# Attention's product with v: plain fp32, two heads in the two column halves of the array, instead of high and low parts over the full array

## The chip, the cores and the metric

The kernel is one program on one core of a Trainium2 chip. The metric is the device time of one execution in microseconds (us); lower is better. A core has TensorE (PE in the profile, with its weight loads shown apart as PEld), VectorE (DVE), ScalarE (ACT), GpSimd (POOL) and a queue engine (SP) that issues transfers. Each engine works through its own list of instructions in the order in which the built program holds them.

## What is computed

Two layers of a diffusion backbone are computed for 128 prompt tokens and 512 sample tokens. Layer 0 is gated attention with 16 query heads and 4 key/value heads of 64 columns; layer 1 is a bidirectional state-space mixer, which the change doesn't touch. The part that matters:

```python
def attend(q, k, v):                      # 16 query heads, 4 kv heads, head_dim 64
    s = einsum('bqgrd,bsgd->bgrqs', qb, k) * scale
    p = softmax(s, axis=-1)
    return einsum('bgrqs,bsgd->bqgrd', p, v)
# prompt tokens see 128 keys; sample tokens see 128 cached keys and 512 own keys
yp = (attend(...) * silu(g)) @ w_out
```

## The kernel before

The tokens lie in five tiles of 128: tile 0 is the prompt, tiles 1 to 4 are the sample. Products are made in the format fp32r, with each operand split into a high part (a cast on ACT) and a low part (source minus high part, on DVE or POOL): `split` is lines 72 to 74, so that these casts and subtractions all bear the lines L73 and L74, and the tile's name tells them apart (`ph`, `pl` for turned probabilities, `qs` for queries, `wh`, `wl` for weights, `v` for v).

`attention` runs over the four kv groups. A group has nine units: four heads with query tiles 1 and 2, the prompt with all four heads, four heads with query tiles 3 and 4. A unit has a first half, `head_A`: the scores of one head and one query tile against all 640 keys (L630), the row maximum (L633, DVE), the exponential (L637, ACT). Its second half is `head_B`: the probabilities of both query tiles are turned in three steps of up to two key tiles each (L658, transposes into the PSUM tile `pt`, of which there are two), split into `ph` and `pl`, and multiplied with `v2` (L668). `v2` holds the high and the low part of v side by side, 2 x 64 columns, so that one matmul of 128 stationary columns makes both products; the two halves of the result lie on different partitions and `combine` (L567 on ACT, L568 on DVE) adds them. The prompt's unit does the same with 128 keys (L598, L606, L607). The gate is scaled, turned (L562) and multiplied in `post`.

The second half of a unit is written between the first half of the next one and other work, the "fill": projections of the next group's queries and of the gate (L283), modulation rows of both layers (L175, plain fp32 in column quarters of the array), and in the last group early pieces of the output projection (L841). The builder's scheduler then sets the final order on each engine; `order` below is that final order.

The array's column halves are used by this kernel already in layer 1, in `diag` (L1145): each program line there multiplies plain fp32 with 64 stationary columns, heads alternating between the two halves, eight matmuls to a tile and group, 160 in all.

## Time and profile before

| what | value |
|---|---|
| median of 3 runs | 988.72 us (988.35 to 992.33) |
| profiled execution, its own time | 996.43 us |
| its span in the trace | 994.6 us |
| granted TensorE clock over the span | 0.979 of full |
| attention's units, first score to last product with v | about 91 to 381 us |

A profiled execution is one execution with the hardware profiler on. Its time stands 7.7 us above the median of the runs, so that differences are worked out against its own rows and then set against the median. Busy times of PE are the union of bars; a bar holds the matmul's passage through the array and ends later than the next matmul may start, so that matmuls of one kind show their true cost in the distance from start to start.

### The profile page before, as it was taken

To read this page: it belongs to the slowest core of one execution; us is meant where nothing else is said; L and a number is where in the kernel's file an instruction comes from. 1 tells how busy PE (TensorE), PEld (TensorE's weight loads), DVE (VectorE), ACT (ScalarE), POOL (GpSimd) and SP (SyncE) were. 2 spreads that over 40 slices of the span, in tenths; PEclk is the share of its full clock that TensorE was granted. 3 is DMA by queue.
4 is the path that set the end of the run, shared out by engine and by line. 5 is a ranking of instruction groups with operands and counts; after the bars stand their busy time and mean duration, and the time that the engine had idled before them with its cause. 6 is when DMAs were issued, how large, how long until landed. Compare 5 with 4: busy or idle time off the path is not lost.

```text
span 994.6 us, 17413 instructions
## 1 busy us (share of the span) xinstructions
PE 933.1 (94%) x6578; PEld 845.7 (85%) x6578; DVE 663.8 (67%) x1046; ACT 517.4 (52%) x1208; POOL 411.8 (41%) x397
## 2 busy tenths in 40 slices
PE   5998999999999989989899989999999999989898
PEld 3887979979997779989799979799889899768686
DVE  4468666566675774884858776856686657898553
ACT  5345666667675763333446565456436552544340
POOL 3245235227271071364235676448543862332000
PEclk9899999999999999999999999999999999999899
DMA  9941253131114223333449766755476545456742
GB/s 307 348 143 50 84 165 128 47 103 36 29 44 128 85 66 109 124 107 89 128 139 264 199 197 198 183 181 157 155 206 189 183 132 160 145 180 206 256 161 101
DMA packets 121476, 146.98 MB, mean 148 GB/s; under 512 B 8688, under 2 KB 93808, under 8 KB 121392
## 3 DMA queue, kind: packets, MB, share of 16 engines
q1 hardware_dynamic: 110640, 140.62, 46.0%
q10 hardware_dynamic: 10752, 5.24, 1.8%
q8 instruction: 52, 0.85, 0.4%
q14 instruction: 32, 0.26, 0.1%
HBM read 128.73 MB, written 17.10 MB: 147 GB/s over the span
## 4 chain that ended last, share of the span: by engine, by line
PE 55%; DVE 16%; DMA 12%; issue 6%; POOL 5%; ACT 5%; SPq 1%; ACTq 0%; POOLq 0%; DVEq 0%
PE pj L914 15%; PE pp L283 8%; DMA am<-acd 5%; PE pj L1383 3%; PE po L668 3%; PE acc L379 3%; PE a L841 3%; PE S L630 3%; PE pt L658 3%; DVE wl L74 2%; DMA u<-yzd 2%; PE pp L175 2%; PE a L1383 2%; POOL am L1132 2%; PE a L1192 2%
## 5 line engine op out<-in xcount | busy, mean ns | idle before, releaser
L914 PE MATMUL pj<-h,wh 128*128 128x322 f32 (+1 forms) x1248 | 289.9, 319 | 10.0 <-DVE B L1006 4.5
L914 PEld LDWEIGHTS pj<-h,wh 128*128 128x128 f32 (+1 forms) x1248 | 210.8, 189 | 19.2 <-issue 12.0
L74 POOL TENSOR_TENSOR wl<-raw,wh 128x512 fp32r<-128x512 f32 (+1 forms) x70 | 134.9, 1938 | 178.7 <-ACT wh L73 178.4
L914 PE MATMUL pj<-h,wl 128*128 128x322 f32 (+1 forms) x624 | 200.6, 322 | 0.0
L73 ACT CAST wh<-raw 128x1024 fp32r<-128x1024 f32 (+1 forms) x117 | 103.2, 912 | 91.3 <-DMA raw<-in_l_w_out 27.9
L1131 ACT ACTIVATE am<-am,nb 128x128 f32<-128x128 f32 x320 | 98.1, 390 | 57.6 <-POOL am L1127 46.2
L914 PEld LDWEIGHTS pj<-h,wl 128*128 128x128 f32 (+1 forms) x624 | 118.4, 190 | 4.2 <-issue 3.8
L283 PE MATMUL pp<-wh,big 128*128 128x256 f32 x576 | 112.2, 285 | 0.5 <-ACT sg L527 0.5
L74 DVE TENSOR_TENSOR wl<-raw,wh 128x1024 fp32r<-128x1024 f32 x47 | 66.7, 1428 | 40.9 <-ACT wh L73 40.9
L283 PEld LDWEIGHTS pp<-wh,big 128*128 128x128 f32 x576 | 91.2, 188 | 0.9 <-ACT sg L527 0.7
L283 PE MATMUL pp<-wl,big 128*128 128x256 f32 x288 | 81.2, 282 | 0.0
L74 DVE TENSOR_TENSOR pl<-pt,ph 128x512 fp32r<-128x512 f32 (+1 forms) x100 | 59.2, 599 | 25.6 <-ACT ph L73 25.0
L633 DVE TENSOR_REDUCE nm<-S 128x1 f32<-128x640 f32 x64 | 52.4, 820 | 13.7 <-PE S L630 12.7
L73 ACT CAST ph<-pt 128x512 fp32r<-128x512 f32 (+1 forms) x100 | 51.4, 518 | 18.8 <-PE pt L658 14.1
L1132 POOL TENSOR_TENSOR am<-am,am 128x1024 f32<-128x1024 f32 x20 | 49.2, 2458 | 22.5 <-ACT am L1131 22.5
L637 ACT ACTIVATE Pt<-S,nm 128x640 f32<-128x640 f32 x64 | 51.3, 803 | 13.1 <-PE pt L658 9.5
L1383 PE MATMUL pj<-wh,h 128*128 128x512 f32 x160 | 54.0, 412 | 2.1 <-ACT wh L73 2.1
L283 PEld LDWEIGHTS pp<-wl,big 128*128 128x128 f32 x288 | 54.3, 188 | 0.0
L630 PE MATMUL S<-kT,qT 128*128 128x320 f32 x256 | 51.4, 326 | 2.3 <-ACT Pt L637 2.3
L658 PE MATMUL pt<-cst,Pt 128*128 128x128 f32 x320 | 50.7, 275 | 2.7 <-DVE pl L74 2.3
L1126 POOL TENSOR_SCALAR_AFFINE_SELECT am<-am 128x1024 f32<-128x1024 f32 x20 | 23.5, 1176 | 59.0 <-DMA am<-acd 51.5
L841 PE MATMUL a<-wh,big 128*128 128x256 f32 x256 | 46.8, 283 | 0.0
(345 smaller groups left out, 2114.9 us busy)
## 6 DMA issues: line engine op xcount, KB each, us to landing
raw<-in_l_w_in SPq DMA_DIRECT2D x48, 512.0 KB
am<-acd SPq DMA_DIRECT2D x40, 512.0 KB
raw<-in_l_w_out SPq DMA_DIRECT2D x36, 512.0 KB
og<-in_l_mod_w SPq DMA_DIRECT2D x29, 512.0 KB
E<-ecd SPq DMA_DIRECT2D x64, 128.0 KB
raw<-in_l_w_in SPq DMA_DIRECT2D x25, 256.0 KB
mw<-in_l_mod_w SPq DMA_DIRECT2D x11, 512.0 KB
ys<-dud SPq DMA_DIRECT2D x20, 256.0 KB
```

The lines of the kernel that those rows point to most:

```text
L73: (heng.tensor_copy if heng else self.nc.scalar.copy)(hi, src)
L74: (eng or self.nc.vector).tensor_tensor(lo, src, r32(hi), op=ALU.subtract)
L283: nc.tensor.matmul(ps, a[:, k, cs], b[:, k, :], start=k == 0 and a is hi and b is w[0], stop=k == KD - 1 and a is lo)
L630: nc.tensor.matmul(S[:, 192 + 320 * q:512 + 320 * q], qTs[g, t][:, h, :], kT[:, hl, 320 * q:320 * q + 320], start=hl == 0, stop=hl == 1)
L633: nc.vector.tensor_reduce(c["m"], c["s"], axis=AX.X, op=ALU.max, negate=True)
L637: nc.scalar.activation(Pt, c["s"], AF.Exp, bias=c["m"], scale=1.0, accum_out=rss[g][t][:, h:h + 1])
L658: nc.tensor.transpose(pt[:, 2 * i + j, :], Pts[j][:, kt * P:kt * P + P], self.ident)
L841: self.nc.tensor.matmul(ps, self.ohl[a][:, k, ts], w[b][:, k, :], start=k == 0 and i == 0, stop=k == KD - 1 and i == 2)
L914: nc.tensor.matmul(ps[0:m, 190 + 322 * half:512 + 322 * half], w[b][:, k, off:off + m], hT[s][:, k, 322 * half:322 * half + 322], start=fi ...
L1131: nc.scalar.activation(af[d][:, h, :], af[d][:, h, :], AF.Exp, bias=self.nb[:, t, i:i + 1], scale=1.0)
L1132: nc.gpsimd.tensor_tensor(af[0], af[0], af[1], op=ALU.add)
L1383: nc.tensor.matmul(self.PS[t][n], y[a][:, kk, :], b, start=k0 + k == 0 and i == 0, stop=k0 + k == 15 and i == 2)
```

## The change

The product with v is no longer split. `v2` and its splits go (L73, L74 on `v`); the stationary operand is the 64 columns of v as they lie in `kv`. Units are formed anew: a unit is now a pair of heads and one query tile, and after two units (two query tiles) the turned probabilities of both heads and both tiles stand in three plain fp32 tiles, `ph0`, `ph1` and `ph2` (key tiles 0 and 1, 2 and 3, 4). They are copied out of PSUM by one instruction each, `ph0` and `ph2` by ACT, `ph1` by DVE. `ph0` has two buffers, the others one. `pv` then multiplies, for each key tile, head 0 into partitions 0 to 63 and head 1 into 64 to 127 of `po`, 10 matmuls with 64 stationary columns and 256 moving ones; it stands in the second step of the next unit. `combine` becomes one copy on ACT. The prompt's four heads go the same way.

```diff
         def kv_open(g):
             kT = self.tl(kvp, [P, 2, 6 * P], F32R, tag="kT", bufs=2)
-            v2 = self.tl(kvp, [P, 6, 2, HD], F32R, tag="v2", bufs=2)
...
         def kv_part(g, a):
...
-            cs = slice(2 * a, 2 * a + 2)
-            self.split(v2[:, cs, 0, :], v2[:, cs, 1, :], vr[:, cs, gs])
...
-        def combine(o, po, e):
-            a, b = slice(64 * e, 64 * e + 64), slice(64 - 64 * e, 128 - 64 * e)
-            nc.scalar.copy(o[a], po[b])
-            nc.vector.tensor_tensor(o[a], po[a], o[a], op=ALU.add)
+        def vcols(g, kt):
+            return vr[:, kt, HD * g:HD * g + HD]
...
-        def prompt_B(g, Pt):
...
-                ph = self.tl(w2, [P, 4, P], F32R, tag="ph")
-                pl = self.tl(w2, [P, 4, P], F32R, tag="pl")
-                self.split(ph, pl, pt)
+                ph = self.tl(w2, [P, 4, P], tag="ph2", bufs=1)
+                nc.scalar.copy(ph, pt)
...
-                for h in range(4):
-                    nc.tensor.matmul(po[:, h, :], v2, pm[0][:, h, :], start=True, stop=False)
-                    nc.tensor.matmul(po[:, h, :], v2, pm[1][:, h, :], start=False, stop=True)
+                for h in range(4):
+                    e = 64 * (h % 2)
+                    nc.tensor.matmul(po[e:e + 64, h // 2, :], vcols(g, 5), pm[0][:, h, :], start=True, stop=True)
+                nc.scalar.copy(o, po)
...
-        def head_B(g, h, half, Pts):
...
-                    ph = self.tl(w2, [P, 4, P], F32R, tag="ph")
-                    pl = self.tl(w2, [P, 4, P], F32R, tag="pl")
-                    self.split(ph[:, 0:2 * n, :], pl[:, 0:2 * n, :], pt[:, 0:2 * n, :])
...
-                def pv(kts=kts, pm=pm):
-                    for m in pm:
-                        for i, kt in enumerate(kts):
-                            vv = v2[:, kt].rearrange("p a d -> p (a d)")
-                            nc.tensor.matmul(po, vv, m[:, 2 * i:2 * i + 2, :].rearrange("p a q -> p (a q)"), start=kt == 0 and m is pm[0], stop=kt == 4 and m is pm[1])
+        turned = {}
+        def pair_B(g, pair, t, Pts):
+            tt = (t - 1) % 2
...
+                def turn(kts=kts, s_=s_):
+                    if tt == 0:
+                        turned[s_] = self.tl(w2, [P, len(kts), 2, 2, P], tag=f"ph{s_}", bufs=2 if s_ == 0 else 1)
+                    pt = self.tl(pT, [P, 4, P], tag="pt")
+                    for i, kt in enumerate(kts):
+                        for e in range(2):
+                            nc.tensor.transpose(pt[:, 2 * i + e, :], Pts[e][:, kt * P:kt * P + P], self.ident)
+                    (nc.vector.tensor_copy if s_ == 1 else nc.scalar.copy)(turned[s_][:, :, :, tt, :], pt[:, 0:2 * len(kts), :].rearrange("p (i e) q -> p i e q", e=2))
...
+            def pv():
+                for kt in range(5):
+                    for e in range(2):
+                        nc.tensor.matmul(po[64 * e:64 * e + 64, :], vcols(g, kt), ph[kt // 2][:, kt % 2, e].rearrange("p a q -> p (a q)"), start=kt == 0, stop=kt == 4)
+                nc.scalar.copy(o, po)
...
-        units = [(g,) + u for g in range(NKV) for u in [(h, 0) for h in range(4)] + [("p",)] + [(h, 1) for h in range(4)]]
+        units = [(g,) + u for g in range(NKV) for u in [(0, 1), (0, 2), (1, 1), (1, 2), ("p",), (0, 3), (0, 4), (1, 3), (1, 4)]]
...
-                    steps[j][0]()
-                    ph.append(steps[j][1])
+                    steps[j]()
...
-                if j and ph:
-                    ph.pop(0)()
-            for p_ in posts:
-                p_()
+                if j == 1 and last:
+                    last[0]()
```

The other edits in the diff rename what the functions return and let the rope table of the keys share the buffer `ph2`. Layer 1 and the end of the kernel keep their order of instructions.

The first place is PE in group 0, at the product with v of one piece of work. Before, it is that of head 1 with query tiles 1 and 2 (L668, `po_1429`), with transposes of probabilities (L658), of keys (L550) and of the gate (L562) between.

```order
L668 MATMUL po_1429<-ph_1435,v_134_841 128x256 x2
L550 MATMUL pt_1499<-identr_62,qs_1494 128x128 x4
L668 MATMUL po_1429<-pl_1436,v_134_841 128x256 x2
L668 MATMUL po_1429<-ph_1451,v_134_841 128x256 x2
L658 MATMUL pt_1509<-cst_60,Pt_1339 128x128
L658 MATMUL pt_1509<-cst_60,Pt_1371 128x128
L668 MATMUL po_1429<-pl_1452,v_134_841 128x256 x2
L562 MATMUL pt_1547<-cst_60,sg_1212 128x128
L562 MATMUL pt_1547<-cst_60,sg_1263 128x128
L668 MATMUL po_1429<-ph_1512,v_134_841 128x256
```

In the changed kernel it is that of the second pair of heads with query tiles 1 and 2 (now L657, `po_1495`), with transposes of probabilities (now L645, the prompt's L591), scores (now L619) and modulation rows (L175).

```order
L657 MATMUL po_1495<-ph_260_1379,kv_82 64x256 x4
L645 MATMUL pt_1564<-cst_60,Pt_1407 128x128
L645 MATMUL pt_1564<-cst_60,Pt_1464 128x128
L657 MATMUL po_1495<-ph_264_1393,kv_82 64x256 x4
L175 MATMUL pp_1660<-og_1661,sT_190 32x512 x2
L591 MATMUL pt_1570<-cst_60,Pt_1497 128x128 x4
L175 MATMUL pp_1660<-og_1665,sT_190 32x512 x2
L619 MATMUL S_1724<-kT_840,qT_1136 128x320 x4
L657 MATMUL po_1495<-ph_274_1459,kv_82 64x256 x2
```

The ten matmuls of one product, which the source writes in one run, stand in pieces of 4, 4 and 2 with full-width work between them. Over the whole program the 160 matmuls of L657 and the prompt's 16 of L599 stand in 49 pieces, most of them 4, 4 and 2 (or 8 and 2); at six places a piece ends between the two heads of a key tile. The rows of L175 stood in 19 pieces in the attention, and stand in 17 now.

The second place is DVE ahead of the first unit, where the keys are rotated (L488, L487, L490) and the first group's v is split (L74 on `v`). Before:

```order
L500 TENSOR_TENSOR kv_82<-qn_805,kw_767 128x256
L74 TENSOR_TENSOR v_134_841<-kv_82,v_134_841 128x2x64 x2
L74 TENSOR_TENSOR v_264_1404<-kv_82,v_264_1404 128x2x64
L488 TENSOR_TENSOR kv_82<-qn_815,ph_778 128x256
L488 TENSOR_TENSOR kv_82<-qn_828,ph_778 128x256
L74 TENSOR_TENSOR v_264_1404<-kv_82,v_264_1404 128x2x64
L74 TENSOR_TENSOR v_134_841<-kv_82,v_134_841 128x2x64
```

In the changed kernel:

```order
L500 TENSOR_TENSOR kv_82<-qn_805,kw_767 128x256
L488 TENSOR_TENSOR kv_82<-qn_815,ph_114_778 128x256
L488 TENSOR_TENSOR kv_82<-qn_828,ph_114_778 128x256
L487 TENSOR_TENSOR qsq_817<-qn_815,ph_114_778 128x8x16 x2
L472 TENSOR_REDUCE qss_834<-qsq_825 128x4
L490 TENSOR_TENSOR kv_82<-kv_82,qsq_817 128x256
```

The splits of v are gone there (six of them for groups 0 and 1, and six later ones), and the rotation follows directly.

## Rows read from the trace of the kernel before

**Rows 1.** The page, busy time of PE over the whole span.
```profile
PE 933.1 (94%) x6578; PEld 845.7 (85%) x6578; DVE 663.8 (67%) x1046; ACT 517.4 (52%) x1208; POOL 411.8 (41%) x397
```

**Rows 2.** Busy time in four stretches: keys and first queries, then the attention.
```profile
core 0: us, PE busy (x) PEld busy (x) DVE busy (x) ACT busy (x) POOL busy (x), PEclk, DMA share, GB/s
66.00:100.00 34.00, 28.64 (x224) 26.44 (x224) 29.20 (x66) 17.36 (x47) 21.99 (x30) 0.95 0.25 72
100.00:200.00 100.00, 98.75 (x798) 88.56 (x798) 63.31 (x139) 67.48 (x165) 33.18 (x44) 1.00 0.33 107
200.00:300.00 100.00, 97.65 (x786) 91.49 (x785) 68.61 (x149) 68.79 (x175) 49.69 (x68) 1.00 0.17 51
300.00:382.00 82.00, 76.11 (x547) 64.26 (x546) 53.39 (x111) 51.24 (x130) 23.12 (x36) 0.98 0.30 95
```

**Rows 3.** Waits of PE from 100 to 382 us: total us, times, longest us.
```profile
PE pt L658 <- DVE pl L74: 2.3, 5, 0.7
PE po L668 <- DVE pl L74: 2.0, 5, 0.7
PE S L630 <- ACT Pt L637: 1.5, 3, 0.9
PE pt L550 <- DVE pl L74: 0.9, 2, 0.7
```

**Rows 4.** The chain that ended last, one piece: start us, us, what.
```profile
144.40 0.95 PE po L668 x8
```

**Rows 5.** Groups by shape on PE, 100 to 382 us (busy us, mean ns).
```profile
L658 PE MATMUL pt<-cst,Pt 128*128 128x128 f32 x320 | 50.7, 275 | 2.7 <-DVE pl L74 2.3 <-ACT kT L551 0.3
...
L668 PE MATMUL po<-ph,v 128*128 128x256 f32 x160 | 39.0, 309 | 0.8 <-ACT ph L73 0.5 <-DVE o L568 0.2
L668 PE MATMUL po<-pl,v 128*128 128x256 f32 x160 | 38.0, 303 | 2.2 <-DVE pl L74 2.0
...
L606 PE MATMUL po<-ph,v 128*128 128x128 f32 x16 | 3.7, 267 | 0.0
```

**Rows 6.** Timeline of PE in layer 1, plain fp32 over the full array.
```profile
525.08 0.94 PE L1186 MATMUL a<-B,h 128*128 128x128 f32 x7
525.86 1.02 PE L1192 MATMUL a<-xw,T 128*128 128x512 f32 x2
```

**Rows 7.** Timeline of PE in layer 1 around one run in column halves.
```profile
619.13 0.31 PE L914 MATMUL pj<-h,wl 128*128 128x322 f32 x1
619.28 0.46 PE L914 MATMUL pj<-h,wh 128*128 128x322 f32 x2
619.67 1.09 PE L1145 MATMUL a<-am,xt 128*64 128x128 f32 x16
620.69 0.41 PE L914 MATMUL pj<-h,wl 128*128 128x322 f32 x1
620.94 0.46 PE L914 MATMUL pj<-h,wh 128*128 128x322 f32 x2
```

**Rows 8.** Line 1145: durations in ns (least, median, most), first and last start.
```profile
L1145 PEld LDWEIGHTS a<-am,xt x320: 132/137/231, 534.2 to 892.8; 128*64 128x64 f32 x160
L1145 PE MATMUL a<-am,xt x320: 272/273/477, 534.2 to 892.9; 128*64 128x128 f32 x160
```

**Rows 9.** Timeline of PE in the attention around a run in column quarters.
```profile
307.53 0.65 PE L658 MATMUL pt<-cst,Pt 128*128 128x128 f32 x4
308.11 1.05 PE L175 MATMUL pp<-raw,sT 128*32 128x512 f32 x4
309.09 0.66 PE L658 MATMUL pt<-cst,Pt 128*128 128x128 f32 x4
```

**Rows 10.** Timeline of DVE where the first groups' v is split.
```profile
71.46 1.06 DVE L74 TENSOR_TENSOR v<-kv,v 128x128 fp32r<-128x128 f32 x3
72.44 1.42 DVE L488 TENSOR_TENSOR kv<-qn,ph 128x256 f32<-128x256 f32 x2
73.79 1.07 DVE L74 TENSOR_TENSOR v<-kv,v 128x128 fp32r<-128x128 f32 x3
```

**Rows 11.** Splits of turned probabilities, 100 to 382 us, on DVE and ACT.
```profile
L74 DVE TENSOR_TENSOR pl<-pt,ph 128x512 fp32r<-128x512 f32 x68 | 45.9, 684 | 13.4 <-ACT ph L73 12.8
L73 ACT CAST ph<-pt 128x512 fp32r<-128x512 f32 x68 | 39.5, 587 | 15.4 <-PE pt L658 13.0 <-DVE o L568 0.7 <-PE pt L598 0.5
```

**Rows 12.** Plain copies out of PSUM by DVE and ACT, durations in ns.
```profile
L345 DVE COPY x<-pt x5: 684/692/692, 11.0 to 19.8; 128x512 f32<-128x512 f32 x5
L345 ACT COPY x<-acc x5: 565/585/586, 11.4 to 19.3; 128x512 f32<-128x512 f32 x5
```

More of the change, by code (lines that the diff above doesn't have):

```diff
@@ L616, in post, with pair_A, score @@
                     sgT = gate_T(g, [0], pair)
[L617 to L621 removed]
+                    nc.vector.tensor_tensor(oT[g][:, pair, 0:P], sgT[:, 0, :], o[:, pair, :], op=ALU.mult)
+            return [turn], pv, post
+        def pair_A(g, pair, t):
+            kT = kvs[g]
             out, Pts = [], []
[L623 removed]
+            for h in (2 * pair, 2 * pair + 1):
                 c = {}
[L626 removed]
+                def score(h=h, c=c):
                     S = self.tl(pS, [P, 1024], tag="S")
@@ L688, in attention, with post @@
+            def post():
+                for u in (t - 1, t):
+                    scaled_gate(g, u, pair)
+                sgT = gate_T(g, (t - 1, t), pair)
+                nc.vector.tensor_tensor(oT[g][:, pair, P * t - P:P * t + P], sgT[:, 0:2].rearrange("p a q -> p (a q)"), o, op=ALU.mult)
+            return steps, pv, post
         GQ, GG = 0, D + 512
@@ L768, in attention @@
             ex()
-        posts = []
-        fill = []
+        last, fill = None, []
         for i, u in enumerate(units):
```

80 lines of the change are left out of this document (23 added, 57 removed).

## The prediction

> **What bounds the kernel now.** I read the busy times first, then the attention by stretches, then who waits. PE is busy for 94% of the span [rows 1]. In the attention's first two stretches, 100 to 300 us, its bars leave 3.6 us free of 200; from 300 to 382 us, the last group, which has no next group to project for, they leave 5.9 of 82. DVE and ACT are busy for two thirds of these stretches [rows 2]. So for three groups out of four the stage lasts as long as PE's own list, and work taken from DVE or ACT is worth only what PE waited for it. The list of PE's waits says how much that is: three of its lines name DVE's subtraction `pl`, 5.2 us in 12 waits, and the exponentials have 1.5 us in 3 more [rows 3]. A bar hides the start of each such wait, because it outlasts the slot of its matmul: a transposing matmul of 275 ns [rows 5] is followed by the next after 109 (four in 0.65 us, less the last bar, [rows 9]), so 0.16 us go unseen in each wait. The waits on `pl` thus cost 5.2 + 12 x 0.16 = 7.1 us.
>
> Ahead of the attention it is another picture: from 66 to 100 us DVE is busy for 29.2 us of 34 and PE for 28.6 [rows 2]; there DVE's list, in which six splits of v stand, delays the first scores.
>
> **The change part by part.** I sum in PE's time, since PE is the bound.
>
> *Removed from PE.* 320 matmuls of 256 columns with `ph` and `pl` [rows 5], at 0.95 / 8 = 0.119 us from start to start [rows 4]: 38.1 us. The prompt's 32 (16 with `ph`, [rows 5], as many with `pl`) at about 0.11, the distance of 128-column records (seven in 0.94 us, less the last bar of 0.27, [rows 6]): 3.5. Together **-41.6**.
>
> *Added to PE.* Layer 1 already has this form. Its 160 program matmuls of L1145 are 320 records [rows 8]: a plain fp32 matmul goes through the array twice. 16 records, that is eight matmuls or four pairs, run in 1.09 us, 0.82 without the last bar [rows 7]; full-width 128-column records need 0.11 each [rows 6], which would be 1.7. So the two column halves do run at the same time, and a pair costs two passes, not four. A pass grows with the moving columns: 0.11 us for 128, 1.02 - 0.59 = 0.43 for 512 [rows 6], so 0.216 for 256. 80 pairs x 2 x 0.216 = 34.6 us; the prompt's 8 pairs x 2 x 0.11 = 1.7; the six places of the built order where a piece ends between the heads leave two halves unpaired, four at 0.43 and two prompt ones at 0.22, 2.2. Together **+38.5**. Two fp32 passes in half the width are thus hardly cheaper than two fp32r passes over the full width: the array's time falls by 3 us, not by half.
>
> *The change of width.* Going into column halves and out again costs time of its own. In layer 1 the last full-width matmul ahead of such a run starts at 619.28 + 0.15 = 619.43 and the second one behind it at 620.94: 1.51 us, of which the run's eight passes are 0.87 and the two full-width ones 2 x 0.15 [rows 7]. That leaves 0.34. In the attention, around a run in quarters, the last transposing matmul starts at 307.91 and the second one behind at 309.26: 1.35 us less two passes of 0.43 and two slots of 0.109 leaves 0.28 [rows 9]. I take 0.31, with both as bounds. The source has 20 runs, but the built order has 49 pieces with full-width work around each: 49 x 0.31 = **+15.2** (13.7 to 16.7). The Trainium skill, "TensorEngine Tiling (Array Packing)", Key Properties, says that changing the tiling mode, not merely the tile, drains TensorE. By that rule each piece pays a drain on the way in and one on the way out; taking a drain as the part of a bar behind its slot, 0.16 us, the sum would be 49 x 2 x 0.16 = 15.7 instead of 15.2.
>
> *L175.* Its pieces fall from 19 to 17, and some quarters that ran two by two now run four by four, four passes fewer: -(2 x 0.31 + 4 x 0.43) = **-2.3**.
>
> PE's list alone therefore becomes longer: -41.6 + 38.5 + 15.2 - 2.3 = **+9.8 us**.
>
> *v's splits.* Six subtractions in two pieces of 1.06 us stand in DVE's list while it is the bound, one ahead of the keys' rotation L488 and one behind it [rows 10]. Up to 2.1 us; **-1.5**, because POOL (22 of 34 us busy there, [rows 2]) also has a link in that chain. Bounds 0 and -2.1. The six later splits lie under PE's work and count for nothing; without that cover they would be 2 us again.
>
> *The splits of p.* DVE loses 68 subtractions of 0.68 us and 32 shorter ones and gains 32 copies of 0.69; ACT's casts of 0.59 become copies of 0.58 [rows 11, 12]. `pt` is freed after one instruction instead of two in a row, and `pv` stands one unit behind its data. So the 7.1 us of waits on `pl` go. The exponentials' waits (1.5 + 3 x 0.16 = 2.0) halve, since DVE's reductions come sooner: 1.0. In the last group the clock stood at 0.98 of full on average, 1.6 us of 82 [rows 2]; with half of its gaps closed I take back half, 0.8. And what PE waits for shorter than the list shows I put at 1.6 us, a quarter of the 5.9 free in the last group. Together **-10.5**, between -3.5 (half of `pl`'s waits) and -16 (`pl`, exponentials, all 5.9 free, and the clock's 1.0 beyond).
>
> *New waits.* `ph1` and `ph2` have one buffer: the copy for the next pair must wait for `pv`, and PE's transposes wait for the copy. A piece of `pv` can also come up ahead of its copy, 0.58 us on ACT behind an exponential. No row shows either; a wait on `pl` cost 0.7 us at most [rows 3]. Nothing if each comes late enough; with one such wait in a third of the 16 products, 4 us. I take **+1.5**, nearer to nothing because the pieces stand behind the next unit's transposes.
>
> Sum: 9.8 - 1.5 - 10.5 + 1.5 = -0.7 us. The profiled execution's 996.4 would become 995.7; the median of the runs lies 7.7 lower, and 988.7 - 0.7 gives **988.0 us**. Layer 1 and the output projection are PE's too, in the same order, so what the attention gains or loses arrives at the end. A measurement of this kernel tells about 0.5%, 4.9 us, from no change.
>
> **The rivals.**
> *The gaps close (faster).* The gains from DVE and ACT reach the -16, v's splits give 2.1 and no new wait comes: 9.8 - 2.1 - 16 = -8 us, 980 us; with each change of width at its lower bound 979. For it: all four groups lose half of DVE's chain, and the last group, with 5.9 us free, has most to give. Against it: from 100 to 300 us there is next to nothing to close. Also here belongs the case that the width's change costs nothing between pieces that stand close, as if a product were one run: 20 runs would save 9 us, 979. 0.33.
> *The pieces aren't covered (slower).* PE's list is 9.8 us longer, and the waits gone are replaced by waits on the new single buffers: with 3.5 regained, 1.0 of v and 4 of new waits, +9.3, 998 us. It decides from where less than 3.4 us net comes back from DVE and ACT. For it: the 3.6 us free in 200. Against it: twelve named waits on an instruction that no longer exists. 0.19.
> *The halves don't overlap at 256 columns (slower).* Then the 80 pairs cost 69 us instead of 35 and the time is 1023. Against it: the rows of L1145 at 128 columns and those of L175 at 512. 0.03.
> *Weight loads aren't hidden (slower).* Loads of 137 ns in front of 176 passes would be 24 us, 1012 us. Against it: 16 loads and 16 passes of L1145 share 0.82 us [rows 7, 8]. 0.02. The Trainium skill, "TensorE: Matmul & The Clock Gate", Part 3, says that a load overlaps matmuls in flight only where the row group differs, which column halves don't; the trace shows them overlapped all the same.
>
> **How the numbers follow.** No measurable change 0.43, faster 0.33, slower 0.19 + 0.03 + 0.02 = 0.24. The likeliest gives 988. For the range the terms at their good ends give 9.8 - 1.5 - 2.1 - 16, so 979, at their bad ends 9.8 + 1.5 - 0 - 3.5 + 4, so 1000.5; I take 978 to 1000, which leaves out the last two rivals and the outer tails. The middle case's own range is 984 to 993.
>
> **What would show it.** Right: records of L657 in pairs a few ns apart, pairs of passes 0.216 us from each other; about 0.3 us more than the slots at each of 49 pieces; no waits on `pl`, PE's bars fuller in the last group; DVE's busy time in the attention down by 24 us or more (45.9 for the long subtractions, less 32 copies of 0.69), with the end of the attention within 5 us of 381. Wrong: pieces that cost much less or more than 0.3 us, PE waiting at L657 or L645 for the copies, or first scores no earlier than 91 us. Most doubtful is how much of DVE's and ACT's relief PE turns into time.

## The result: about 1% slower, and the profile after

The changed kernel takes 1000.6 us (median of 5 runs, 999.0 to 1004.8) where the kernel before takes 990.4 (5 runs, 988.4 to 994.9): a ratio of 1.010, with a 95% interval of 1.0074 to 1.0126. Measured again on another occasion it was 1.0114 (1.0077 to 1.0152). The forecast was 988 us, between 978 and 1000, so the sign was missed and the time lies just above the range.

The profile after shows PE's share unchanged against [rows 1], with less work on DVE and ACT:

```profile
PE 937.1 (94%) x6578; PEld 823.1 (82%) x6578; DVE 610.0 (61%) x926; ACT 487.0 (49%) x1144; POOL 413.7 (41%) x397
```

The same stretches as in [rows 2], busy time by engine:

```profile
66.00:100.00 34.00, 31.16 (x238) 29.12 (x238) 29.46 (x69) 17.10 (x42) 20.38 (x28) 0.91 0.23 69
100.00:200.00 100.00, 98.41 (x783) 79.97 (x782) 43.21 (x93) 54.65 (x139) 33.33 (x42) 1.00 0.31 102
200.00:300.00 100.00, 97.93 (x759) 81.96 (x759) 50.70 (x109) 58.19 (x154) 40.33 (x56) 1.00 0.15 48
300.00:382.00 82.00, 77.39 (x551) 57.12 (x550) 39.20 (x78) 43.75 (x117) 32.87 (x48) 0.98 0.37 123
```

From 100 to 382 us DVE has 52 us less to do (133.1 against 185.3) and ACT 31 us less. PE's bars are as full as before. PE's waits in the same 282 us, as in [rows 3]:

```profile
PE pj L206 <- ACT xn L73: 2.4, 1, 2.4
PE S L619 <- ACT Pt L626: 1.2, 4, 0.6
PE pt L559 <- DVE og L606: 1.2, 1, 1.2
PE pt L645 <- ACT kT L548: 0.7, 1, 0.7
PE pp L175 <- ACT sg L527: 0.7, 2, 0.5
```

The waits on `pl` are gone, the product L657 waits for nothing, and other waits have come. The largest is at the passage into the output projection, where 94 of the 96 early output matmuls now stand behind the last piece of the product (24 before). Lines of PE's timeline there, with the wait and what it was for in brackets:

```profile
366.16 1.95 PE L657 MATMUL po<-ph,kv 128*64 128x256 f32 x16
368.04 0.44 PE L559 MATMUL pt<-cst,sg 128*128 128x128 f32 x2
368.40 0.65 PE L657 MATMUL po<-ph,kv 128*64 128x256 f32 x4
371.44 0.73 PE L206 MATMUL pj<-xn,selr 128*128 128x512 f32 x2 [2.38 <-ACT xn L73]
```

The pieces cost what the forecast said. One of them on PE's timeline:

```profile
112.39 0.38 PE L645 MATMUL pt<-cst,Pt 128*128 128x128 f32 x2
112.70 1.08 PE L657 MATMUL po<-ph,kv 128*64 128x256 f32 x8
113.71 0.39 PE L283 MATMUL pp<-wl,big 128*128 128x256 f32 x1
113.94 0.40 PE L283 MATMUL pp<-wh,big 128*128 128x256 f32 x2
```

The second transposing matmul starts at 112.39 + 0.11 = 112.50, the second full-width one behind the piece at 113.94: 1.44 us. Eight records are four matmuls, two pairs, four passes of 0.216; with the two full-width slots (0.11 and 0.118) that is 1.09, and 0.35 is left for the change of width. Worked out in this way for all 49 pieces the median is 0.34 and the sum 14.8 us (one 2.4 us wait behind the last piece taken off).

**Where to measure.** The time of one execution varies by several us at both ends, so I compare the stretch that holds the change: from the last kv projection (L379) to the last matmul of layer 0's output projection. Both ends stand in the rows of the source lines, as the second of the two starts. A second profile of the kernel before, then the changed kernel:

```profile
L379 PE MATMUL acc<-vh,big x80: 276/280/367, 30.2 to 63.2; 128*128 128x256 f32 x80
L841 PE MATMUL a<-wh,big x256: 274/282/370, 381.5 to 431.8; 128*128 128x256 f32 x128
L630 PE MATMUL S<-kT,qT x256: 302/309/632, 88.7 to 359.3; 128*128 128x320 f32 x128
```
```profile
L379 PE MATMUL acc<-vh,big x80: 276/280/367, 29.7 to 62.7; 128*128 128x256 f32 x80
L813 PE MATMUL a<-wh,big x256: 278/282/384, 387.5 to 437.1; 128*128 128x256 f32 x128
L619 PE MATMUL S<-kT,qT x256: 302/309/475, 85.6 to 359.1; 128*128 128x320 f32 x128
```

Before it is 368.7 us in these two profiles and 369.5 in a third, after 374.4, 374.9 and 374.7 in three (the third of each moves one instruction of layer 1, behind the stretch): **4.9 to 6.2 us more, repeatable to 0.8 us**. The rest of the 10 us arises behind it, in layer 1, whose order on PE the change does not touch; it is treated at the end of the experiments.

The granted clock has a part in these lengths. The trace shows it at one of two levels, full (2.4 GHz) or half (1.2 GHz). Between the first score and the end of the stretch the kernel before is at half clock once (356.6 to 360.0 us in the second profile), the changed kernel twice (88.9 to 92.4 and 372.2 to 375.7); the third profile of the kernel before also has two such times (88.2 to 91.6 and 357.8 to 361.2), and it is the one of 369.5. Three projection matmuls at half clock take 0.64 us from start to start instead of 0.35 (L283 in the run without the splits of p, below), so one such time costs up to 1.6 us. With two on both sides the changed kernel is 4.9 to 5.4 us behind.

### The profile page after: what moved, and what is told of

Same layout as the page of the kernel before. It is cut to its first block, busy times and chain, and to the rows that moved or that the text cites. A ratio compares the mean times of both kernels' runs of the same rounds, so it can differ in the third digit from the quotient of the medians.

```text
span 998.0 us, 17116 instructions
## 1 busy us (share of the span) xinstructions
PE 937.1 (94%) x6578; PEld 823.1 (82%) x6578; DVE 610.0 (61%) x926; ACT 487.0 (49%) x1144; POOL 413.7 (41%) x397
## 4 chain that ended last, share of the span: by engine, by line
PE 50%; DMA 13%; DVE 13%; issue 10%; POOL 6%; ACT 6%; SPq 1%; POOLq 0%; ACTq 0%; DVEq 0%
PE pj L886 13%; PE pp L283 7%; DMA am<-acd 5%; PE pj L1355 3%; PE acc L379 3%; PE S L619 3%; PE a L813 3%; PE po L657 3%; DMA u<-yzd 2%; PE pt L645 2%; DVE wl L74 2%; ACT am L1103 2%; PE pp L175 2%; POOL am L1104 2%; PE a L1355 2%
## 5 line engine op out<-in xcount | busy, mean ns | idle before, releaser
L886 PEld LDWEIGHTS pj<-h,wh 128*128 128x128 f32 (+1 forms) x1248 | 211.6, 190 | 16.7 <-issue 11.9
L74 POOL TENSOR_TENSOR wl<-raw,wh 128x512 fp32r<-128x512 f32 (+1 forms) x70 | 135.1, 1941 | 173.3 <-ACT wh L73 152.1
L73 ACT CAST wh<-raw 128x1024 fp32r<-128x1024 f32 (+1 forms) x117 | 103.4, 912 | 90.3 <-DMA raw<-in_l_w_out 29.7
L283 PE MATMUL pp<-wh,big 128*128 128x256 f32 x576 | 113.6, 287 | 0.5 <-ACT sg L527 0.3
L283 PEld LDWEIGHTS pp<-wh,big 128*128 128x128 f32 x576 | 91.7, 190 | 4.0 <-issue 2.3
L74 DVE TENSOR_TENSOR wl<-raw,wh 128x1024 fp32r<-128x1024 f32 x47 | 66.2, 1417 | 39.3 <-ACT wh L73 39.2
L283 PE MATMUL pp<-wl,big 128*128 128x256 f32 x288 | 82.0, 285 | 0.0
L283 PEld LDWEIGHTS pp<-wl,big 128*128 128x128 f32 x288 | 54.7, 190 | 1.2 <-issue 1.2
L619 PE MATMUL S<-kT,qT 128*128 128x320 f32 x256 | 52.9, 332 | 1.8 <-ACT Pt L626 1.2
L645 PE MATMUL pt<-cst,Pt 128*128 128x128 f32 x320 | 50.8, 278 | 1.0 <-ACT kT L548 0.7
L619 PEld LDWEIGHTS S<-kT,qT 128*128 128x128 f32 x256 | 38.7, 192 | 12.4 <-issue 5.2
L657 PE MATMUL po<-ph,kv 128*64 128x256 f32 x320 | 45.7, 392 | 0.0
```

The source lines that it names most:

```text
L73: (heng.tensor_copy if heng else self.nc.scalar.copy)(hi, src)
L74: (eng or self.nc.vector).tensor_tensor(lo, src, r32(hi), op=ALU.subtract)
L283: nc.tensor.matmul(ps, a[:, k, cs], b[:, k, :], start=k == 0 and a is hi and b is w[0], stop=k == KD - 1 and a is lo)
L619: nc.tensor.matmul(S[:, 192 + 320 * q:512 + 320 * q], qTs[g, t][:, h, :], kT[:, hl, 320 * q:320 * q + 320], start=hl == 0, stop=hl == 1)
L645: nc.tensor.transpose(pt[:, 2 * i + e, :], Pts[e][:, kt * P:kt * P + P], self.ident)
L657: nc.tensor.matmul(po[64 * e:64 * e + 64, :], vcols(g, kt), ph[kt // 2][:, kt % 2, e].rearrange("p a q -> p (a q)"), start=kt == 0, stop=k ...
```

## The experiments

Theory L: PE's list became longer by the changes of width, and too little waiting came back for it. Theory T: the attention proper came out even, and the loss is in the passage to the output projection. The expectations call the stretch above "the stretch". Ratios are to the kernel before on the same chip, with 95% intervals; the kernel before against itself gave 0.997 (0.9946 to 0.9999), so a few thousandths say nothing.

### The kernel before once more

> The kernel before, unchanged, for a second profiled execution: the first lay 6 us above the median of its runs, so it may not be a typical one. Theory L (PE's list): the change makes PE's list about 9.8 us longer and nothing comes back for it; then the time from the last kv projection L379 to the first output matmul of out0 is about 10 us shorter here than in the changed kernel (324.8 us), so about 315 us. Theory T (the transition): the attention proper came out even, and the loss arises only where the attention passes into the output projection, in PE's idle time and half clock of 369 to 388 us; then the last score of this run stands where that of the first profile stood against the last L379 (296.2 us behind it, changed kernel 296.4).

The stretch is 368.7 again, with the first score 25.5 us behind L379 and the last one 296.1. The first profile of the kernel before was a long one only outside it: L379 ended 2.4 us later, and the part behind the stretch took 560.4 us instead of 557.4. The last score of the changed kernel lies 296.4 behind L379, as theory T has it; but its last pv stands 94 early output matmuls earlier in the list, so equal scores there do not yet mean equal work done. The next runs decide.

### The splits of p alone, then those of v as well

```diff
-                    ph = self.tl(w2, [P, 4, P], F32R, tag="ph")
-                    pl = self.tl(w2, [P, 4, P], F32R, tag="pl")
-                    self.split(ph[:, 0:2 * n, :], pl[:, 0:2 * n, :], pt[:, 0:2 * n, :])
-                    pm.extend((ph, pl))
+                    ph = self.tl(w2, [P, 4, P], F32R, tag="ph")
+                    nc.scalar.copy(ph[:, 0:2 * n, :], pt[:, 0:2 * n, :])
+                    pm.extend((ph, ph))
```

> The kernel before, without the subtractions of p: ph stands in the place of pl in the second product (the output then has twice the rounded part; PE's matmuls stay the same in number and shape). This is the forecast's term for the splits of p alone, on an unchanged PE list. The forecast: 10.5 us faster, between 3.5 and 16, so 980 us (974 to 987). Theory L: less than that, 2 to 5 us faster, 985 to 988, because where PE no longer waits on pl it waits at the next thing in line (the last group's gates, the split of the output's operand). Theory T: the full 10.5, since the loss lies elsewhere.

Measured: 988.3 us, ratio 0.9956 (0.9928 to 0.9984); the stretch 363.05, **5.6 us less, not 10.5**. (The medians show less of it: 988.3 against 990.4 for the unchanged kernel beside it.) What PE waited for then, from 88 to 427 us:

```profile
PE pt L522 <- DVE qs L74: 2.7, 4, 1.3
PE pt L522 <- DVE qss L472: 2.7, 1, 2.7
PE S L629 <- ACT Pt L636: 1.6, 2, 1.2
PE pj L206 <- ACT xn L73: 1.3, 1, 1.3
PE pp L175 <- DMA raw<-in_l_mod_w: 1.0, 1, 1.0
```

No `pl` is left in it, and still the bars leave as much free as before: behind the first score up to the end of the stretch 10.5 us, where the kernel before had 10.8. Waits of 0.7 us on `pl` made room for fewer and longer ones on other things. (The one on `qss` stands ahead of the first score, as it did in the kernel before.) The granted clock, the number behind POOL's, has no part in the gain, since the time at half clock only stands elsewhere; the kernel before (second profile), then this one:

```profile
62.00:100.00 38.00, 32.57 (x257) 30.14 (x256) 32.47 (x75) 20.91 (x53) 24.09 (x32) 0.96 0.31 94
300.00:388.00 88.00, 82.21 (x594) 70.26 (x594) 54.40 (x113) 51.22 (x130) 21.27 (x34) 0.98 0.31 102
```
```profile
62.00:100.00 38.00, 33.34 (x255) 31.30 (x254) 32.38 (x75) 21.16 (x53) 24.35 (x33) 0.91 0.28 84
300.00:388.00 88.00, 81.26 (x628) 72.38 (x627) 41.02 (x84) 52.69 (x135) 27.02 (x41) 1.00 0.33 108
```

What was gained shows when each distance from one start on PE to the next, behind the first score, is set against the slot, the distance of back-to-back records of that shape. The listed waits with their hidden parts fell from 14.5 us in 25 waits to 13.0 in 15; the gaps too short for that list fell from 7.5 us to 3.3, and 4.2 of the 5.6 us lie there.

```diff
-            self.split(v2[:, cs, 0, :], v2[:, cs, 1, :], vr[:, cs, gs])
+            nc.scalar.copy(v2[:, cs], vr[:, cs, gs].unsqueeze(2).to_broadcast([P, 2, 2, HD]))
```

> The kernel before without the subtractions of p, as in the run that had those alone, and without those of v too: one cast writes the rounded v into both halves (the output then lacks the remainders). Without p's alone the stretch took 363.0 us and the first score stood 25.6 us behind the last L379. Forecast's term for v: 1.5 us. If the 2.6 us that the changed kernel gains to its first score are v's and stay, 22.9 to the first score and 360.4 for the stretch. If what comes early only waits later, as it did when v's subtractions were placed late, 362 to 363.

Measured: 989.4 us, 0.999 (0.997 to 1.001). The first score comes 22.9 us behind L379, 2.6 earlier, and the stretch is 364.3, **1.3 longer than with v's splits**. PE's timeline shows why; the kernel before (second profile), then this one:

```profile
85.43 0.28 PE L283 MATMUL pp<-wh,big 128*128 128x256 f32 x1
88.32 0.54 PE L522 MATMUL pt<-identr,qs 128*128 128x128 f32 x4 [2.60 <-DVE qss L472]
88.70 0.82 PE L630 MATMUL S<-kT,qT 128*128 128x320 f32 x4
```
```profile
86.57 0.41 PE L629 MATMUL S<-kT,qT 128*128 128x320 f32 x1 [0.25 <-ACT qT L523]
89.39 0.51 PE L522 MATMUL pt<-identr,qs 128*128 128x128 f32 x4 [2.40 <-DVE qs L74]
89.73 0.67 PE L629 MATMUL S<-kT,qT 128*128 128x320 f32 x3
```

The wait of 2.4 to 2.6 us for the next queries is still there. It stood ahead of the first score and now stands behind it: the milestone moved, the wait did not. In the changed kernel the same wait, 2.40 us, stands at 88.5.

### v's splits moved instead of removed

```diff
+            self.tc.keep_in_program_order(nc.vector.tensor_tensor(v2[:, cs, 1, :], src, r32(v2[:, cs, 0, :]), op=ALU.subtract))
...
+        for a in range(3):
+            v_part(0, a)
```

> The kernel before with the splits of v kept, but DVE's subtractions for the first group's v placed behind the first scores (and each later group's behind what stands ahead of it in the source). This takes v's splits out of the chain to the first scores and leaves PE's list as it was. The forecast's term for them: 1.5 us less, at most 2.1. The changed kernel's profile says 2.6: there the first score stands 22.9 us behind the last L379, without the change 25.5. If that difference is v's, here 22.9 as well and 2.6 us less in all: a stretch of 366.1 us and a median some 0.26% below before. If it was something else's (the single buffer of the rope table, the order of the scheduler), 25.5 and no change.

22.9 us to the first score, as expected, and a stretch of 372.3, 3.6 longer than before; 1.0021 (0.9994 to 1.0049). The early start came to nothing here too. Behind the first score this run is at half clock three times (from 90.7, 124.9 and 363.8 us), the kernel before once; counted from start to start, that takes 4.3 us instead of 1.1, and waits take 18.6 instead of 14.5. How much of the loss is the splits' late place is not separated.

### The changed kernel again

> The changed kernel, unchanged, on the same chip as the others, for more runs and a second profiled execution. In the first two profiles of the kernel before, the stretch from the last kv projection L379 to the last matmul of layer 0's output projection took 368.7 us both times, in the changed one 374.4, so 5.7 us more, while the medians lie 10 us apart; the stretches ahead of it and behind it vary by some 2 us each from execution to execution. Theory L (PE's list is longer by the changes of width, and too little waiting comes back): 374.4 again to within 0.5 us, and a median 5 to 8 us above that of the kernel before. If the other 4 us are the change's as well, the stretch behind is again 3 us longer than the 557 to 560 seen without it.

Stretch 374.9, ratio 1.0114. The part behind is again longer, 560.7 us.

### The wait in front of the output projection

```diff
-            if i == 2:
+            if i == 0:
                 for k in range(4, 6):
-                    self.mod_gate(0, k, self.grow[0, k], pj, "pj", wk, "xn", "xn", 2)
+                    self.mod_gate(0, k, self.grow[0, k], pj, "pj", wk, "xn", "xn", 2, True)
...
+            if late:
+                self.tc.keep_in_program_order(mm)
```

> The changed kernel with the gate's four matmuls of layer 0 (L206, L207) put behind the first 24 matmuls of the output projection, where the changed kernel has them right behind the last pv piece and PE waits 2.4 us there for ACT's xn, after which the granted clock was at half for 3.5 us. If these are a new wait that belongs to the change (PE comes to the end of its list ahead of ACT), the stretch of 374.4 becomes 371 to 372: 2.4 less for the wait, up to 1.7 more for the clock. If PE would only wait for the next thing (the pre copies, POOL's splits of the operand, which end at 377.4), less than 1 us.

Stretch 375.7, 1.0102 (1.0071 to 1.0133): nothing gained. The wait for `xn` is gone, and PE waits at the next matmul:

```profile
PE pp L815 <- ACT pre L700: 4.5, 3, 3.6
```

2.4 us at L206 became 3.6 at the early output matmuls. This is against theory T: the wait there is not a separate loss that could be mended on the spot.

### The product without column halves

```diff
-                for kt in range(5):
-                    for e in range(2):
-                        nc.tensor.matmul(po[64 * e:64 * e + 64, :], vcols(g, kt), ...)
+                for e in range(2):
+                    for kt in range(5):
+                        nc.tensor.matmul(po[:, e, :], vwide(g, kt, e), ...)
```

> The changed kernel with each product with v over the full width of the array, one head after the other: v's columns of two neighbouring groups as weights, each head's useful half of the rows copied out (for the first and the last group the neighbour is missing and the wrong columns are taken, which changes the output and not the work). No change of width is left in the product, and every matmul costs its own two passes: 160 x 0.432 + 16 x 0.22 = 72.6 us of PE against 38.7 in the changed kernel's column halves. So the stretch becomes 374.4 + 33.9 less what the 49 changes of width cost there. Theory L, 0.31 each: 393.1 us, some 1016 to 1019 in all. If the pieces cost nothing and the loss lies in new waits alone: 408 us, 1031 or more. If each costs 0.37: 390 us.

Stretch 387.3, 1014.5 us, 1.0238 (1.0202 to 1.0275): 12.7 us more than the changed kernel's 374.6, where the passes alone cost 33.9 more. So 21.2 us came back, 0.43 for each of the 49 pieces. Some of it is waiting (its bars leave 8.7 us free in the stretch behind the first score, the changed kernel's 12.1); without these 3.4 it is 0.36 a piece, and 0.33 without the one time at half clock more that the changed kernel has (some 1.5 us). The halves do run side by side, and the pieces are paid for.

### Fewer pieces and more

Seven kernels change nothing but the order of instructions (the indivisible form also adds two branches to a product), and with it how the product is cut. Priority for the product with its first matmul pinned behind what the source has ahead of it (37 pieces, all early output matmuls ahead of the last one):

```diff
+                    with self.tc.high_priority(offset=150):
+                        last[0]()
...
+                        if kt + e == 0:
+                            self.tc.keep_in_program_order(mm)
```

> The changed kernel with the pv matmuls given priority and each product's first one kept behind what is ahead of it in the source: 37 pieces between full-width work instead of 49, and in the built order all 96 early output matmuls stand ahead of the last pv piece, where the changed kernel has 94 of them behind it. Theory L: 12 pieces fewer at 0.31 us are 3.7 us less, 997 us. Theory T: the transition is mended too, another 3 to 5 us (the 2.4 us wait for xn, the two waits of 0.46 for pre, half of the slow-clock stretch), 992 to 994. Both wrong, and some new wait paid: 1000 or more.

Each product one indivisible section:

```diff
+                with self.tc.tile_critical():
```

> The changed kernel with every product with v issued in one run: 20 pieces instead of 49, 88 of the 96 early output matmuls still behind the last one. A run then waits for all its operands at its start and has two branch instructions around it, which no row prices. Theory L: 29 pieces fewer at 0.31 us are 9.0 us less, 991.6 us, less what the branches and the waits for all operands cost. Theory T: no change from fewer pieces beyond 1 or 2 us, 999 to 1001, as the attention proper is not what lost.

TensorE in the order of the source, in the changed kernel and in the kernel before:

```diff
+        with self.tc.manual_schedule(engines={mybir.EngineType.PE}):
```

> The changed kernel with TensorE's instructions of the attention in the order of the source: each product with v is one run (20 pieces instead of 49), L175 has 17, and all 96 early output matmuls stand ahead of the last product. Theory L: 29 pieces fewer at 0.31 to 0.36 us are 9.0 to 10.4 us, the halves that the pieces' ends left unpaired 2.2 more: 11 to 13 us of PE's list, the stretch from the last L379 to the last output matmul 362 to 364 us instead of 374.4 and some 988 us in all, if the source's order brings no waits that the scheduler's order avoids; each such wait shows as idle time of PE and is to be taken off by its own length. If the pieces are not what costs (each under 0.1 us), no more than 3 us less, 997 or above.

> The kernel before in the same manner, TensorE's instructions of the attention in the order of the source. It has no pieces in its product, so this is the price of the source's order by itself, and beside the kernel above it the change at equal order. Theory L, by the forecast's own terms with 20 pieces in place of 49: list -41.6 + 36.3 + 20 x 0.33 = +1.3 us, less 2.6 us for v and 2 to 6 for p's splits: the change would be 3 to 7 us faster there. Waits on the splits of p should grow here, since in source order the product stands right behind them: the stretch 372 us or more instead of 368.7. If the change's loss had nothing to do with the pieces, the changed kernel stays some 6 us behind this one.

Key tiles in another order, then with priority too, then a small priority that cuts more:

```diff
-                for kt in range(5):
+                for kt in (4, 2, 3, 0, 1):
```

> The changed kernel with one edit: the product takes the key tiles in the order 4, 2, 3, 0, 1, so that its first matmul needs the copy that is made last. In the built order it then has 25 pieces instead of 49 and four unpaired halves instead of twelve; 94 of the 96 early output matmuls still stand behind the last one, and no instruction is taken out. Theory L (the pieces cost 0.31 to 0.36 us each): 24 x 0.31 to 0.36 + 1.3 for the halves are 8.7 to 9.9 us, the stretch from the last L379 to the last output matmul 365 to 366 us instead of 374.4 and 374.9, some 991 us in all, level with the kernel before. If starting later costs waits, less by their length. If the loss is in the transition or in waits on single buffers, 372 or more.

> The same with priority for the product's matmuls in the scheduler: 22 pieces, no unpaired half. Theory L: 27 x 0.31 to 0.36 + 2.2 are 10.6 to 11.9 us, 363 to 364 us for the stretch, some 989 us in all, 1 to 3 us ahead of the kernel before. If priority for the product delays the scores behind it, PE waits in the next unit and the stretch is above that of the kernel without priority.

> The other direction: the changed kernel with a small priority for the product's matmuls, by which the scheduler cuts it into 69 pieces instead of 49, with 32 unpaired halves instead of twelve; nothing else is changed. Theory L: 20 x 0.31 to 0.36 + 4.7 for the halves are 10.9 to 11.9 us more, the stretch 385 to 387 us, some 1011 us in all. If a piece costs nothing by itself and only the unpaired halves do: 379.

Measured, with the stretch in us:

| kernel | pieces | stretch | median | ratio (95%) |
|---|---|---|---|---|
| small priority | 69 | 382.7 | 1007.7 | 1.0147 (1.0114 to 1.0179) |
| changed kernel | 49 | 374.4 to 374.9 | 1000.6 | 1.0114 (1.0077 to 1.0152) |
| pinned | 37 | 372.2 | 992.4 | 1.0014 (0.9989 to 1.0039) |
| other key order | 25 | 373.8 | 994.9 | 1.0017 (0.9991 to 1.0042) |
| the same, with priority | 22 | 371.0 | 998.2 | 1.0037 (1.0010 to 1.0065) |
| indivisible | 20 | 419.0 | 1043.0 | 1.0528 (1.0487 to 1.0569) |
| changed, source order | 20 | 447.4 | 1070.1 | 1.0797 (1.0774 to 1.0820) |
| before, source order | 0 | 463.7 | 1089.3 | 1.1000 (1.0975 to 1.1025) |

With more pieces the stretch grows by 7.9 to 8.4 us of the expected 10.9 to 11.9. With fewer it hardly falls: theory L expected 8.7 to 9.9 us from 25 pieces and got 0.6 to 1.1. The pieces themselves did become cheaper (their changes of width sum to 8.1 us instead of 14.8), but PE's bars leave 16.4 us free in the stretch behind the first score instead of 12.1. The copies of turned probabilities (L646) and who waited for them, changed kernel and then the one with 25 pieces:

```profile
  PE po L657: 3.2, 1
...
  PE pt L559: 0.2, 1
  PE pt L547: 0.2, 1
```
```profile
  PE po L657: 4.7, 6
...
  PE pt L559: 1.9, 2
...
  PE pt L645: 1.4, 4
...
  PE pt L547: 0.2, 1
```

In each list the first line is what the copies waited for, the others who waited for the copies: us, times. A product that is issued whole starts when its last copy is there, and holds `ph1` and `ph2`, which have one buffer, until then. The copies for the next pair waited for it six times instead of once, and PE for the copies 3.5 us in 7 waits instead of 0.4 in 2. That accounts for 3.1 of the 4.3 us. Counted from start to start, all waits with their hidden parts grow by 5.0 us (14.7 in 18 waits to 19.7 in 25), while one time at half clock less gives back some 1.5; about 3 us more of what the cheaper pieces saved went into shorter gaps, and what those waited for stays open. My reading is that an early piece cost 0.34 us and freed a buffer, so that some of it was time that PE would have waited; two buffers for both tags, which would test this, were not tried.

The pinned kernel's median is where theory T had put it (992 to 994), but its stretch fell by 2.1 to 2.6 us, of the 3.7 that theory L had for its pieces alone. Its profiled execution is at half clock three times behind the first score (from 87.1, 124.7 and 240.7 us), so it does not tell the two theories apart.

The two kernels in source order say little of the pieces, since PE waits everywhere (77 us in the changed one), but they show the change at equal order: with 20 pieces it is 16 us faster than without the change. That direction was expected, at 3 to 7 us; most of the 16 are waits and clock, since the bars leave 77 us free instead of 83 and the granted clock over the span is 0.953 against 0.941. In the indivisible form many a run waits long at its start; the releaser named here, a transfer of weights, is nothing that the product reads:

```profile
169.22 4.53 PE L659 MATMUL po<-ph,kv 128*64 128x256 f32 x20 [4.04 <-DMA raw<-in_l_w_in]
```

### What lies behind the stretch

PE's waits in the first 70 us of layer 1, kernel before and changed kernel:

```profile
PE a L1014 <- DVE u L1006: 2.4, 1, 2.4
PE pj L914 <- ACT Wh L984: 2.4, 1, 2.4
```
```profile
PE a L986 <- DVE u L978: 3.7, 1, 3.7
PE pj L886 <- ACT Wh L956: 1.5, 1, 1.5
```

Behind the wait of 3.7 us the granted clock stood at 0.89 on average from 475 to 490 us, against 1.00. The first 400 matmul records behind the stretch took 68.7 and 68.9 us in the two profiles of the kernel before, 70.7 and 70.8 in the changed one. A candidate was a cast of weights that waits for its transfer ahead of an exponential on ACT:

```profile
471.05 1.05 ACT L73 CAST wh<-raw 128x1024 fp32r<-128x1024 f32 x1 [4.60 <-DMA raw<-in_l_w_in]
472.00 0.47 ACT L921 ACTIVATE am<-am 128x320 f32<-128x320 f32 x1
```

```diff
-        nc.scalar.activation(u, u, AF.Exp)
+        self.dt_exp = nc.scalar.activation(u, u, AF.Exp).ins
...
+        with self.tc.issue_after(self.dt_exp):
             lag(x_unit, 0, 2, (x_turn, 0, 1))
```

> The changed kernel with one instruction moved in layer 1, far behind the change: ACT's cast of the third weight tile (wh) now stands behind the exponential of dt_stage (L921) instead of ahead of it. In the changed kernel's profile ACT waits 4.6 us for that tile's transfer there, the exponential behind it is 2.65 us late, DVE's chain with it, PE waits 3.7 us at L986 against 2.4 in the kernel before, and the granted clock is at half for a while after it. That is 2 us which the first 400 matmuls behind the output projection lose beyond the attention (70.7 us against 68.9). If it is the cast in front of the exponential: 68 us or less for these 400, 2 to 4 us less in all, 997 to 998. If PE waits for the weights themselves, or DVE's slow instructions beside POOL set the wait, no change.

> The kernel before with the same one instruction moved. There the exponential (L949) was 1.3 us late behind the cast, and PE waited 2.4 us at L1014. If the cast in front of it is the cause, 1 to 1.5 us less for the first 400 matmuls behind the output projection (68.9 us), 989 to 990 in all, and the two kernels then differ by what the attention loses alone, 5.7 to 6.2 us. If not, no change.

> The changed kernel with the key tiles in the order 4, 2, 3, 0, 1 (25 pieces), which took 994.9 us, and the same instruction of layer 1 moved. There the first 400 matmuls took 70.2 us with waits of 2.4 us at L986 and 2.4 at L886. If the cast in front of the exponential matters in this kernel too, 1 to 1.5 us less, 993 to 994, level with the kernel before; if not, 995.

All three came out without a gain: 1002.4 us, 1.0125 (1.0102 to 1.0148); 991.0, 1.0015 (0.9998 to 1.0032); 994.8, 1.0052 (1.0033 to 1.0071). The exponential came earlier and the wait at L986 fell to 3.1 us, but the 400 records took 71.9, 70.9 and 70.7 us. So this is not the cause. Kernels without the change show the longer start too (71.5 us without the splits of p), so it is not the product's own.

The whole part behind the stretch goes with the granted clock. With half of each time at half clock taken as lost, 10.8, 14.0 and 7.5 us are lost there in the three profiles of the kernel before, whose parts behind are 557.4, 560.4 and 555.7 us long, and 12.5, 14.4 and 14.2 in those of the changed kernel, with 561.0, 560.7 and 560.3. Without this the parts are 546.4 to 548.1 and 546.1 to 548.5: no difference is left. The kernel with the key tiles in another order, 557.1 us with 8.6 lost, is short there for the same reason, and that is most of what it gains on the changed kernel. Whether the change brings the additional time at half clock stays open, since one profile of the kernel before has nearly as much.

## Why the prediction failed, step by step

The stretch, divided at the first score. "Slots" adds up PE's records at the distance of back-to-back ones of their shape (0.110 us for 128 columns, 0.118 for 256, 0.146 for 320, 0.228 for 512, column passes 0.11, 0.216 and 0.43); the changes of width are L175's runs at 0.31 and the pieces as measured; the rest is waiting, clock, and what the slots don't hold.

| us | before | without splits of p | without both splits | changed |
|---|---|---|---|---|
| L379 to first score | 25.5 | 25.6 | 22.9 | 22.9 |
| first score to end of stretch | 343.1 | 337.5 | 341.4 | 351.4 |
| of it slots | 313.4 | 313.4 | 313.7 | 309.4 |
| changes of width | 5.9 | 5.9 | 5.9 | 20.1 |
| rest | 23.8 | 18.2 | 21.8 | 21.9 |

- **PE's list, +9.8: right.** Slots -4.0 (forecast: -41.6 + 38.5, and 4 x 0.43 less for L175), pieces +14.8 (forecast 15.2), two runs of L175 fewer -0.6: +10.2. Against the kernel without either split, whose waits on them are as gone as the changed kernel's, the stretch is 10.0 to 10.5 us longer, and the rest is the same (21.8 and 21.9), though not in its parts: the changed kernel has one time at half clock more, some 1.5 us, and 1.1 us less that the bars leave free. The list arrived in the time nearly whole. That weight loads would hide was right too: eight records of L657 with eight loads of 136 ns fill 1.08 us, four passes and the last bar.
- **The splits of p, -10.5: the step that failed.** Taken away alone they give 5.6. I counted each named wait with its hidden part, half of the waits on exponentials, and a quarter of what was free, as if a wait that ends gave its whole length. PE then stood at the next thing in line, and the listed waits fell by 1.5 us only. Part of the sum stood in it twice: of the 5.9 us free in the last group 3.8 were waits on `pl` and 1.3 on exponentials, already counted, so there was no room for the 1.6 beside them (a quarter of 5.9 is 1.5, at that) nor for the bound of -16. The gaps too short for the list, which I had put at this 1.6, gave 4.2. The 0.8 of clock did not come either: the changed kernel is at half clock twice behind the first score, the kernel before once or twice. The lower bound of 3.5 was the nearer one.
- **v's splits, -1.5: failed.** The first score came 2.6 us earlier, more than forecast, and the end of the stretch not at all. I had priced the milestone, not the wait behind it. Without v's splits the stretch is 1.3 us longer, not shorter.
- **New waits, +1.5: about nothing** beyond what the kernel without splits has as well. The single buffers did not bind, because the product came in pieces; with 25 pieces they did.
- **"What the attention gains or loses arrives at the end": incomplete.** Some 3 us more are lost behind it (560.3 to 561.0 us in three profiles of the changed kernel, 555.7 to 560.4 in three of the kernel before, one of each with the cast moved), and they go with the granted clock.

Together, the two relief terms were to give 12.0 and gave 4.3 (368.7 to 364.3). With the list at +10.2 that is +5.9, as measured in the stretch. This is the rival "the pieces aren't covered", with one correction. It was to decide where less than 3.4 us net came back beside the 1.5 of v's splits, 4.9 in all; 4.3 came back, so its condition held. But its cause was to be new waits on single buffers, and those took next to nothing (0.4 us in 2 waits). That its 998 us is near the measured time is in part luck, since some 3 of the 10 us lie behind the stretch, where it had nothing. The forecast also started from a median of 988.7 us in 3 runs, which 5 runs put at 990.4.

The signs named for right and wrong: DVE's relief (52 us), the vanished `pl` and the price of a piece all came as "right", and the time was wrong all the same. "The end of the attention within 5 us of 381" was a bad sign to choose: the last product ended at 369 because the scheduler had put early output matmuls behind it.

No version here that computes the whole output is shown to beat the kernel before. The changed kernel with the key tiles in another order, or with its product pinned, is level with it (1.0017 and 1.0014), and so about 6 to 10 us better than the change as made, of which the stretch shows 0.6 to 2.6.

## What to carry to other kernels

Where one engine's list is full, work added to that list counts whole, and work taken from other engines counts only for the part of a wait that nothing else fills: take the operation away by itself, in the old kernel, before counting on it. A milestone that comes earlier is no gain until the wait behind it is gone. Pieces of an interleaved product cost a change of width each, but joining them delays the release of the buffers that they read; the two have to be priced together. And where kernels differ by 1%, add up the time at half clock before explaining the rest: here it came and went between executions of one and the same kernel.

## What the runs showed of the hardware

A change of width costs about the same however long the run is: a median of 0.34 us over 49 pieces of one to eight matmuls, 0.33 over 25 of mostly ten. The Trainium skill, "TensorEngine Tiling (Array Packing)", Key Properties, says that a change of tiling mode drains TensorE; the rows agree in that each change costs time, and give the price.

DVE is slowed beside POOL. In the changed kernel a 128 x 256 subtraction `qs` took 1.48 us at 86.83, while POOL's L74 ran from 85.36 to 88.03, and 0.43 at 89.12, when POOL had only an operation on 128 x 4:

```profile
85.36 2.67 POOL L74 TENSOR_TENSOR wl<-raw,wh 128x512 fp32r<-128x512 f32 x2
86.83 1.48 DVE L74 TENSOR_TENSOR qs<-qn,qs 128x256 fp32r<-128x256 f32 x1
```

Of the 23 such subtractions in that trace three took 1.44 to 1.51 us, all begun while POOL subtracted a tile of 128 x 512, and the other 20 took 0.41 to 0.43. The wait of 2.4 us at L522 is behind the one at 86.83. In the kernel before the same two subtractions of POOL met two multiplications of 128 x 128 on DVE (L487), which took 2.55 us at 83.70 instead of the 0.49 of the pair at 80.53; so a wait of this length stood there with and without v's splits.
